# Moving layer norm 1's scale and shift ahead of the transposes, with adds on GpSimd, in an encoder block on one core

## The chip, the core and the metric

The kernel runs on one core of a Trainium2 chip. The metric is device microseconds of one execution, the median of several runs; lower is better. TensorE does the matrix products and the transposes, VectorE (DVE), ScalarE (ACT) and GpSimd (POOL) the work on single elements, SyncE (SP) issues the transfers.

## What is computed

One encoder block on 256 tokens of width 2048 and 16 meta tokens, in float32. The part around the change is the end of the mixer and the start of the feed-forward part:

```python
def layer_norm(x, g, b):
    mu = jnp.mean(xf, axis=-1, keepdims=True)
    var = jnp.mean(jnp.square(xf - mu), axis=-1, keepdims=True)
    y = (xf - mu) * lax.rsqrt(var + LN_EPS)
    return y * g + b
...
        mix = jnp.concatenate([o_hg, o_ret], axis=-1) @ w_out[layer]
        h = layer_norm(DEEPNORM_ALPHA * h + mix, ln1_g[layer], ln1_b[layer])
        ff = (jax.nn.silu(h @ w_gate[layer]) * (h @ w_up[layer])) @ w_down[layer]
        h = layer_norm(DEEPNORM_ALPHA * h + ff, ln2_g[layer], ln2_b[layer])
```

So `h` is needed twice: as the operand of the gate and up products (feature-major, after a transpose) and as the residual of the second sum (token-major, as it comes).

## The kernel before

**Precision.** Each weight block of 128 x 2048 floats is fetched into one of three `raw` buffers and split into a rounded high part `whi` (a cast on ACT, L77) and the rest `wlo` (a subtraction on DVE, L78), three buffers each. Activations are split the same way. A product is then three matmuls: high by high, high by low, low by high.

**Token groups.** `token_group` makes 512 output columns for both tiles of 128 tokens (tile 0 and tile 1). Its argument `order` lists pairs (tile i, weight block g); for each pair TensorE issues 12 matmuls (4 pieces of 128 rows, three matmuls each, L133). After a tile's last pair `evac` reads the sum out of PSUM. After every second piece, that is every six matmuls, `tick()` is called: it takes the next entry of the list `steps` once it has been passed over as many times as the entry's number says.

**Layer norm 1.** After the last quarter of the output projection, `add_up` adds tile i's result into `acc` (token-major) on DVE (L740, L742 for the statistics) and calls `ln1_tile(i)`. That forms mean and variance (L212, L184), the power -0.5 on GpSimd (L186), the shift (L214), and normalizes the four chunks c0 to c3 of 512 columns, in place (L770 on ACT, L218 on DVE). Each chunk then becomes a step: four transposes on TensorE into one PSUM bank (L237), four ACT instructions that scale and shift each 128 columns with a per-partition gain and bias (L227), a cast to the high part of `h` on ACT (L231), a subtraction for the low part on DVE (L232). The residual `acc` gets the same gain and bias a second time, token-major, on DVE, by the entries of `later` (L777, L778) with rows of gain and bias that were copied to all partitions (`gb`).

**Gate and up.** `first_hidden` runs a token group for the first 512 columns of gate, in the order (0,0), (0,1), (0,2), (1,0), (1,1), (1,2), (0,3), (1,3), then one for up. The chunks of tile 1 are transposed while TensorE works on tile 0 of the gate group.

**Order.** A scheduling pass fixes the order on each engine when the program is built; on the chip each engine works through its own list strictly in that order and waits where an operand is not ready.

Of the kernel before, what the change touches and what calls it, by code (L numbers as in the profile page):

```python
# [9 lines left out]
F32 = mybir.dt.float32  # L10
# [3 lines left out]
ALU = mybir.AluOpType  # L14
AX = mybir.AxisListType

P = 128
# [14 lines left out]
ALPHA = 2.0 ** 0.25  # L32
# [3 lines left out]
C_LB, C_HG, C_RG, C_RB, C_IG, C_IB, C_1G, C_1B = 0, 16, 24, 32, 40, 56, 72, 88  # L36
# [4 lines left out]
def encoder_kernel(ctx: ExitStack, tc: tile.TileContext, x, meta, par, rows, w_in, w_out,  # L41
                   w_gu, w_down, masks, rope, dtab, out):
    nc = tc.nc
# [9 lines left out]
    def bank(c):  # L53
        return pss.tile([P, 512], F32, name="sc") if c % 2 else psm.tile([P, 512], F32, name="ms")


    def fetch(src, parts=1):
        raw = rawp.tile([P, 2048], F32, name="raw")
        w = 2048 // parts
        for p in range(parts):  # L60
            nc.sync.dma_start(raw[:, p * w:(p + 1) * w], src[:, p * w:(p + 1) * w])
        return raw, parts
# [1 line left out]
    def new_split():  # L64
        return (splitp.tile([P, 2048], F32R, name="whi"), splitp.tile([P, 2048], F32R, name="wlo"))

    def split(fetched, dst=None):
        hi, lo = dst or new_split()
        split_parts(fetched, hi, lo, 0, 2048)
        return hi, lo  # L70

    def split_parts(fetched, hi, lo, c0, c1):
        raw, parts = fetched
        w = 2048 // parts
        for c in range(c0, c1, w):
            sl = slice(c, c + w)
            nc.scalar.copy(hi[:, sl], raw[:, sl])  # L77
            nc.vector.tensor_tensor(out=lo[:, sl], in0=raw[:, sl], in1=hi[:, sl].bitcast(F32), op=ALU.subtract)  # L78

    def load_block(src):  # L80
        return split(fetch(src))


    soon, steps = [], deque()
# [18 lines left out]
    def token_group(blocks, operand, order, evac, split_of=None, halve=False):  # L103

        ps = [psp.tile([P, 512], F32, name="pp") for _ in range(2)]
        ws, left, seen = {}, [sum(1 for t, _ in order if t == i) for i in range(2)], [0, 0]
        for i, g in order:  # L110
            if g not in ws:
                ws[g] = split_of(g) if split_of else load_block(blocks[g])
            whi, wlo = ws[g]
            left[i] -= 1
            if halve and i:
                if left[i]:
                    continue
                n = len(ws)
                for half in range(2):
                    ph = psp.tile([P, 512], F32, name="pp")  # L120
                    for k in range(4 * n):
                        a_hi, a_lo = operand(i, k)
                        c = (k % 4) * 512 + half * 256
                        for m, (a, w) in enumerate(((a_hi, 0), (a_hi, 1), (a_lo, 0))):
                            nc.tensor.matmul(ph[:, :256], a, ws[k // 4][w][:, c:c + 256],  # L125
                                             start=(k == 0 and m == 0), stop=(k == 4 * n - 1 and m == 2))
                    evac(i, ph[:, :256], half)
                continue
            for j in range(4):
                k = 4 * g + j  # L130
                a_hi, a_lo = operand(i, k)
                for m, (a, w) in enumerate(((a_hi, whi), (a_hi, wlo), (a_lo, whi))):
                    nc.tensor.matmul(ps[i], a, w[:, j * 512:(j + 1) * 512],  # L133
                                     start=(seen[i] == 0), stop=(left[i] == 0 and j == 3 and m == 2))
                    seen[i] = 1
                if j % 2:
                    tick()
            if left[i] == 0:
                if halve:
                    evac(i, ps[i][:, :256], 0)  # L140
                    evac(i, ps[i][:, 256:], 1)
                else:
                    evac(i, ps[i])
# [33 lines left out]
    ident = cpool.tile([P, P], F32, name="ident")  # L177
# [32 lines left out]
    def moments(mom, rstd, shift, st, np_):  # L210

        nc.vector.bn_aggr(out=mom[:np_], in_=st[:np_])  # L212
        rsqrt(rstd[:np_], mom[:np_, 1:2], 1, np_, LN_EPS)
        nc.vector.tensor_scalar(out=shift[:np_], in0=mom[:np_, 0:1], scalar1=rstd[:np_], scalar2=-1.0,  # L214
                                op0=ALU.mult, op1=ALU.mult)
# [18 lines left out]
    def transposed_chunk(src, c, pool, cg, cb, hs, ls, on_act):  # L234
        pt = bank(c)
        for k in range(4):
            nc.tensor.transpose(pt[:, k * P:(k + 1) * P], src[:, (4 * c + k) * P:(4 * c + k + 1) * P], ident)  # L237
        affine_split(pt, pool, cg, cb, c, hs, ls, on_act)
# [126 lines left out]
    with tc.tile_pool(name="att", bufs=1) as att:  # L365
# [349 lines left out]
        acc, gb = big[:, :2], big[:, 2:]  # L715
# [21 lines left out]
        def add_up(n, scale, stats, done=None):  # L737
            def evac(i, ps):
                sl = acc[:, i, n * 512:(n + 1) * 512]
                nc.vector.scalar_tensor_tensor(out=sl, in0=sl, scalar=scale, in1=ps, op0=ALU.mult, op1=ALU.add)  # L740
                if stats:
                    nc.vector.bn_stats(out=lst[:, i, n, :], in_=sl)  # L742
                if done:
                    done(i)
            return evac
# [11 lines left out]
    ffp = ctx.enter_context(tc.tile_pool(name="ffp", bufs=1))  # L757
    hp = ctx.enter_context(tc.tile_pool(name="hp", bufs=1))
    h = hp.tile([P, KC, 2, SEQ], F32R, name="h")

    later = []

    def ln1_tile(i):
        moments(lm[:, i], lr[:, i], ls[:, i], lst[:, i, :4], P)
        for c in range(4):
            sl = acc[:, i, c * 512:(c + 1) * 512]
            if i == 0 and c < 2:
                normalize(sl, sl, lm[:, i, 0:1], lr[:, i])
            else:
                nc.scalar.activation(sl, sl, AF.Identity, scale=lr[:, i], bias=ls[:, i])  # L770

        def chunk(c):
            transposed_chunk(acc[:, i], c, ffp, C_1G, C_1B, h[:, 4 * c:4 * c + 4, 0, i * P:(i + 1) * P], h[:, 4 * c:4 * c + 4, 1, i * P:(i + 1) * P], 4)

        def affine(c):
            sl = slice(c * 512, (c + 1) * 512)
            nc.vector.tensor_tensor(out=acc[:, i, sl], in0=acc[:, i, sl], in1=gb[:, 0, sl], op=ALU.mult)  # L777
            nc.vector.tensor_tensor(out=acc[:, i, sl], in0=acc[:, i, sl], in1=gb[:, 1, sl], op=ALU.add)  # L778
        steps.append((3, lambda: chunk(0)))
        for c in range(1, 4):  # L780
            steps.append((1, lambda c=c: chunk(c)))
        later.extend((2, lambda c=c: affine(c)) for c in range(4))

    row_bcast(2, gb[:, 0])
    row_bcast(3, gb[:, 1])
    with tc.tile_pool(name="spare", bufs=1) as spare:
        def held(g):
            dst = None
            if g == 3:
                dst = (spare.tile([P, 2048], F32R, name="shi"), spare.tile([P, 2048], F32R, name="slo"))  # L790
            return split(fetch(w_out[12 + g]), dst)

        def done(i):
            ln1_tile(i)
        token_group(None, halves(mhi, mlo), [(0, 0), (1, 0), (0, 1), (0, 2), (0, 3), (1, 1), (1, 2), (1, 3)],
                    add_up(3, ALPHA, True, done), held)
    hid = [actp.tile([P, 2, 8, SEQ], F32R, name=f"t{i}", tag="mix", bufs=2) for i in range(2)]
    fpool = ctx.enter_context(tc.tile_pool(name="fpool", bufs=1))
    hid.append(fpool.tile([P, 2, 8, SEQ], F32R, name="t2"))
# [27 lines left out]
    def first_hidden():  # L827

        gate = [None, None]

        def gate_evac(i, ps):
            gate[i] = g = ffp.tile([P, 512], F32, name="gate", tag="w", bufs=6)
            nc.scalar.activation(g, ps, AF.Sigmoid)
            nc.vector.tensor_tensor(out=g, in0=ps, in1=g, op=ALU.mult)

        def up_evac(i, ps):
            t = gate[i]
            nc.vector.tensor_tensor(out=t, in0=ps, in1=t, op=ALU.mult)

            def turn():  # L840
                pt = bank(i)
                for k in range(4):
                    nc.tensor.transpose(pt[:, k * P:(k + 1) * P], t[:, k * P:(k + 1) * P], ident)
                pv = pt.rearrange("p (k t) -> p k t", k=4)
                hi = hid[0][:, 0, :4, i * P:(i + 1) * P]
                nc.scalar.copy(hi, pv)
                nc.vector.tensor_tensor(out=hid[0][:, 1, :4, i * P:(i + 1) * P], in0=pv, in1=hi.bitcast(F32),
                                        op=ALU.subtract)
            soon.append([2, turn])
        token_group([w_gu[g] for g in range(4)], h_op,  # L850
                    [(0, 0), (0, 1), (0, 2), (1, 0), (1, 1), (1, 2), (0, 3), (1, 3)], gate_evac)
        steps.extend(later)
        token_group([w_gu[4 + g] for g in range(4)], h_op, alternate(4), up_evac)

    def hidden(f, s):
# [158 lines left out]
```

## Time and profile before

| | |
|---|---|
| median of 3 runs | 1289.88 us (1289.38 to 1291.33) |
| the profiled execution, own time | 1288.35 us |
| its span on the core | 1286.6 us |
| TensorE busy | 98% of the span |
| DVE, ACT, GpSimd busy | 59%, 43%, 1% |

The profiled execution lies 1.5 us below the median. TensorE is busy for nearly all of the span, so what counts in any other engine's work is only where TensorE has to wait for it. Chunk names c0 to c3 and tile numbers below are those of the section above; "gate group" is the token group of the first gate columns.

### The profile page before, as it was taken

What the parts mean: (1) busy time and instruction counts of PE and PEld (TensorE: products, weight loads), DVE (VectorE), ACT (ScalarE), POOL (GpSimd) and SP (SyncE); (2) the same over time, 40 slices, a digit from 0 to 9 for tenths busy, and PEclk for the clock granted to TensorE, in tenths of its full rate; (3) what the DMA queues carried; (4) which work ended last, traced back from release to release, by engine and by line L of the source; (5) the groups of instructions that cost most, each with busy time, mean ns of one, the idle gap of its engine ahead of it and who ended that gap; (6) DMA issues with size and microseconds to landing.
All of it is one profiled execution on the core that took longest, in us unless ns stands there. A gap on an engine that the chain in (4) does not pass through costs nothing.

```text
span 1286.6 us, 17123 instructions
## 1 busy us (share of the span) xinstructions
PE 1261.6 (98%) x7260; PEld 1111.8 (86%) x7260; DVE 757.9 (59%) x888; ACT 554.0 (43%) x586; POOL 13.6 (1%) x26
## 2 busy tenths in 40 slices
PE   6999999999999999999999999999999999999996
PEld 4989999898999888878888888888888888888886
DVE  7765575565566685775555555444455555554565
ACT  7634434443444343564444444433344444444340
POOL 0000000000000000000000000000000000000000
PEclk9999999999999999999999999999999999999998
DMA  6644444444434477465555555555555555555541
GB/s 234 252 154 161 164 159 139 162 164 164 164 136 160 154 304 256 169 235 198 189 197 195 180 185 194 184 189 190 192 208 184 194 197 186 181 189 191 190 175 66
DMA packets 34956, 237.53 MB, mean 185 GB/s; under 512 B 4016, under 2 KB 4656, under 8 KB 6960
## 3 DMA queue, kind: packets, MB, share of 16 engines
q1 hardware_dynamic: 34880, 236.44, 51.9%
q8 instruction: 57, 0.93, 0.3%
q14 instruction: 19, 0.16, 0.0%
HBM read 234.33 MB, written 2.10 MB: 184 GB/s over the span
## 4 chain that ended last, share of the span: by engine, by line
PE 95%; DVE 2%; ACT 1%; issue 1%; DMA 0%; POOL 0%; SPq 0%; POOLq 0%; DVEq 0%
PE pp L133 33%; PE pp L863 23%; PE pp L321 15%; PE pp L868 12%; PE pp L332 5%; PE pp L337 2%; PE sc L463 1%; PE pp L125 1%; PE sc L645 1%; DMA raw<-in_w_in_dram 0%; DVE wlo L78 0%; ACT fl L227 0%; PE ms L575 0%; PE ms L572 0%; PE ms L657 0%
## 5 line engine op out<-in xcount | busy, mean ns | idle before, releaser
L78 DVE TENSOR_TENSOR wlo<-raw,whi 128x2048 fp32r<-128x2048 f32 (+1 forms) x211 | 478.8, 2270 | 390.1 <-ACT whi L77 382.7
L77 ACT CAST whi<-raw 128x2048 fp32r<-128x2048 f32 (+1 forms) x211 | 399.5, 1893 | 407.4 <-PE pp L133 201.1
L863 PE MATMUL pp<-h,whi 128*128 128x512 f32 x1280 | 305.4, 391 | 0.0
L863 PEld LDWEIGHTS pp<-h,whi 128*128 128x128 f32 x1280 | 235.3, 188 | 45.6
L133 PE MATMUL pp<-whi,t 128*128 128x512 f32 x648 | 200.0, 389 | 0.0
L321 PE MATMUL pp<-xx,whi 128*128 128x272 f32 x1024 | 199.7, 290 | 0.0
L868 PEld LDWEIGHTS pp<-h,wlo 128*128 128x128 f32 x1280 | 164.0, 191 | 6.2
L868 PE MATMUL pp<-h,wlo 128*128 128x256 f32 x1280 | 166.1, 283 | 0.0
L321 PEld LDWEIGHTS pp<-xx,whi 128*128 128x128 f32 x1024 | 162.3, 188 | 0.5
L321 PE MATMUL pp<-xx,wlo 128*128 128x272 f32 x512 | 146.8, 287 | 0.0
L133 PEld LDWEIGHTS pp<-whi,t 128*128 128x128 f32 x648 | 121.6, 188 | 25.3
L133 PE MATMUL pp<-wlo,t 128*128 128x512 f32 x324 | 126.1, 389 | 0.0
L321 PEld LDWEIGHTS pp<-xx,wlo 128*128 128x128 f32 x512 | 96.5, 188 | 0.2
L133 PE MATMUL pp<-whi,xx 128*128 128x512 f32 x256 | 85.6, 405 | 2.0 <-ACT xx L231 1.9
L133 PEld LDWEIGHTS pp<-wlo,t 128*128 128x128 f32 x324 | 60.8, 188 | 12.5
L332 PE MATMUL pp<-xx,whi 128*128 128x512 f32 x256 | 63.5, 396 | 0.0
L133 PEld LDWEIGHTS pp<-whi,xx 128*128 128x128 f32 x256 | 48.9, 192 | 13.5 <-ACT xx L231 2.8
L332 PEld LDWEIGHTS pp<-xx,whi 128*128 128x128 f32 x256 | 47.0, 188 | 9.0
L133 PE MATMUL pp<-wlo,xx 128*128 128x512 f32 x128 | 51.0, 398 | 0.1
L133 PE MATMUL pp<-whi,mhi 128*128 128x512 f32 x120 | 46.9, 391 | 0.0
L133 PE MATMUL pp<-whi,mlo 128*128 128x512 f32 x120 | 46.7, 389 | 0.0
L133 PE MATMUL pp<-wlo,mhi 128*128 128x512 f32 x120 | 46.7, 389 | 0.0
(207 smaller groups left out, 996.9 us busy)
## 6 DMA issues: line engine op xcount, KB each, us to landing
raw<-in_w_gu_dram SPq DMA_DIRECT2D x88, 1024.0 KB, 4.9
raw<-in_w_in_dram SPq DMA_DIRECT2D x62, 1024.0 KB, 4.9
raw<-in_w_down_dram SPq DMA_DIRECT2D x44, 1024.0 KB, 4.9
raw<-in_w_out_dram SPq DMA_DIRECT2D x16, 1024.0 KB, 4.9
acc<-in_rows_dram SPq DMA_DIRECT2D x6, 1024.0 KB, 7.4
raw<-in_w_in_dram SPq DMA_DIRECT2D x4, 512.0 KB, 8.3
acc<-in_x_dram SPq DMA_DIRECT2D x2, 1024.0 KB, 6.0
out_dram<-acc SPq DMA_DIRECT2D x6, 256.0 KB, 2.3
```

Source lines behind the costliest of these rows:

```text
L77: nc.scalar.copy(hi[:, sl], raw[:, sl])
L78: nc.vector.tensor_tensor(out=lo[:, sl], in0=raw[:, sl], in1=hi[:, sl].bitcast(F32), op=ALU.subtract)
L125: nc.tensor.matmul(ph[:, :256], a, ws[k // 4][w][:, c:c + 256], start=(k == 0 and m == 0), stop=(k == 4 * n - 1 and m == 2))
L133: nc.tensor.matmul(ps[i], a, w[:, j * 512:(j + 1) * 512], start=(seen[i] == 0), stop=(left[i] == 0 and j == 3 and m == 2))
L321: nc.tensor.matmul(ps[:, :T], w[:, kc, :], a[:, kc, XM:], start=(kc == 0 and j == 0), stop=(kc == KC - 1 and j == 2))
L332: nc.tensor.matmul(ps.rearrange("p (m t) -> p m t", m=2), hi[:, kc, :], xx[:, kc, :, X0:], start=(kc == 0), stop=False)
L337: nc.tensor.matmul(ps[:, :SEQ], lo[:, kc, :], xhi[:, kc, X0:], start=False, stop=(kc == KC - 1))
L463: nc.tensor.matmul(sc[:, c * 192:(c + 1) * 192], K[:, (o + c) * P:(o + c + 1) * P], E[:, :, (o + c) * 64:(o + c + 1) * 64], start=True, st ...
L645: nc.tensor.matmul(sc[:, c0:c0 + n], RK[:, k, k0:k0 + P], RQ[:, k, q0:q0 + n], start=(k == 0), stop=(k == 1))
L863: nc.tensor.matmul(ps, hi[:, kc, :], h[:, kc].rearrange("p m t -> p (m t)"), start=(kc == 0), stop=False)
L868: nc.tensor.matmul(ps[:, :SEQ], lo[:, kc, :], h[:, kc, 0, :], start=False, stop=(kc == KC - 1))
```

## The change

Layer norm 1's gain and bias are applied once, token-major, before the transposes: DVE multiplies each chunk of `acc` by the gain row (L773), and the bias row is added by DVE for c0 and by GpSimd for c1 to c3 (L774). The transposed chunk is then split straight from PSUM: one cast on ACT (L785), one subtraction on DVE (L786). `later` is gone. Only c0 of tile 0 is normalized on DVE, all others on ACT. A chunk's first step waits for four ticks in place of three. The gate group takes all four weight blocks for tile 0, then all four for tile 1; for that, block 3's split goes into a buffer of its own (the later `t2`), behind c0's add on DVE, and block 2 is fetched and split in two halves, with the low part of one half made on GpSimd and the other on DVE. The evacuation of the last quarter of the projection has a higher priority in the scheduling pass.

```diff
-    def split_parts(fetched, hi, lo, c0, c1):
+    def split_parts(fetched, hi, lo, c0, c1, *engines):
...
-            nc.vector.tensor_tensor(out=lo[:, sl], in0=raw[:, sl], in1=hi[:, sl].bitcast(F32), op=ALU.subtract)
+            (engines[c // w] if engines else nc.vector).tensor_tensor(out=lo[:, sl], in0=raw[:, sl], in1=hi[:, sl].bitcast(F32), op=ALU.subtract)
...
-            if i == 0 and c < 2:
+            if i == 0 and c == 0:
                 normalize(sl, sl, lm[:, i, 0:1], lr[:, i])
             else:
                 nc.scalar.activation(sl, sl, AF.Identity, scale=lr[:, i], bias=ls[:, i])
+            nc.vector.tensor_tensor(out=sl, in0=sl, in1=gb[:, 0, cols], op=ALU.mult)
+            m = (nc.gpsimd if c else nc.vector).tensor_tensor(out=sl, in0=sl, in1=gb[:, 1, cols], op=ALU.add)
+            if c == 0:
+                begun[:] = [m.ins]
 
         def chunk(c):
-            transposed_chunk(acc[:, i], c, ffp, C_1G, C_1B, h[:, 4 * c:4 * c + 4, 0, i * P:(i + 1) * P], h[:, 4 * c:4 * c + 4, 1, i * P:(i + 1) * P], 4)
-
-        def affine(c):
-            sl = slice(c * 512, (c + 1) * 512)
-            nc.vector.tensor_tensor(out=acc[:, i, sl], in0=acc[:, i, sl], in1=gb[:, 0, sl], op=ALU.mult)
-            nc.vector.tensor_tensor(out=acc[:, i, sl], in0=acc[:, i, sl], in1=gb[:, 1, sl], op=ALU.add)
-        steps.append((3, lambda: chunk(0)))
+            pt = bank(c)
+            for k in range(4):
+                kc = 4 * c + k
+                nc.tensor.transpose(pt[:, k * P:(k + 1) * P], acc[:, i, kc * P:(kc + 1) * P], ident)
+            pv = pt.rearrange("p (k t) -> p k t", k=4)
+            part = h[:, 4 * c:4 * c + 4, :, i * P:(i + 1) * P]
+            nc.scalar.copy(part[:, :, 0, :], pv)
+            nc.vector.tensor_tensor(out=part[:, :, 1, :], in0=pv, in1=part[:, :, 0, :].bitcast(F32), op=ALU.subtract)
+        steps.append((4, lambda: chunk(0)))
         for c in range(1, 4):
             steps.append((1, lambda c=c: chunk(c)))
-        later.extend((2, lambda c=c: affine(c)) for c in range(4))
...
+        def evac(i, ps):
+            with tc.high_priority():
+                sum_up(i, ps)
...
+        def gate_split(g):
+            flat = hid[2].rearrange("p m k t -> p (m k t)")
+            if g == 2:
+                return split(fetch(w_gu[g], 2), None, nc.gpsimd, nc.vector)
+            if g == 3:
+                with tc.issue_after(begun[0]):
+                    return split(fetch(w_gu[g]), (flat[:, :2048], flat[:, 2048:]))
+            return split(fetch(w_gu[g]))
...
-        token_group([w_gu[g] for g in range(4)], h_op,
-                    [(0, 0), (0, 1), (0, 2), (1, 0), (1, 1), (1, 2), (0, 3), (1, 3)], gate_evac)
-        steps.extend(later)
+        token_group(None, h_op, [(i, g) for i in range(2) for g in range(4)], gate_evac, gate_split)
```

On every engine the order before this stage and after the up group is the same in both programs, and TensorE issues the same number of matmuls and transposes.

On DVE, from tile 0's normalization to tile 1's multiplications, the list before reads as follows (`acc<-acc` at L777 and L778 are the gain and bias of the residual; `h<-fl` is a low part of `h`):

```order
L218 TENSOR_SCALAR acc<-acc,lm,lr 128x512 x2
L777 TENSOR_TENSOR acc<-acc 128x512
L778 TENSOR_TENSOR acc<-acc 128x512
L78 TENSOR_TENSOR wlo<-raw,whi 128x2048
L232 TENSOR_TENSOR h<-fl,h 128x4x128
L777 TENSOR_TENSOR acc<-acc 128x512 x2
L232 TENSOR_TENSOR h<-fl,h 128x4x128
L740 SCALAR_TENSOR_TENSOR acc<-acc,pp 128x512
L778 TENSOR_TENSOR acc<-acc 128x512
L232 TENSOR_TENSOR h<-fl,h 128x4x128
L742 BN_STATS lst<-acc 128x6
L778 TENSOR_TENSOR acc<-acc 128x512
```

In the changed program the same stretch of DVE's list reads:

```order
L773 TENSOR_TENSOR acc<-acc 128x512 x2
L774 TENSOR_TENSOR acc<-acc 128x512
L773 TENSOR_TENSOR acc<-acc 128x512 x2
L78 TENSOR_TENSOR wlo<-raw,whi 128x2048
L786 TENSOR_TENSOR h<-ms,h 128x4x128
L786 TENSOR_TENSOR h<-sc,h 128x4x128
L740 SCALAR_TENSOR_TENSOR acc<-acc,pp 128x512
L78 TENSOR_TENSOR wlo<-raw,whi 128x1024
L742 BN_STATS lst<-acc 128x6
L786 TENSOR_TENSOR h<-ms,h 128x4x128
L212 BN_AGGR lm<-lst 128x2
L786 TENSOR_TENSOR h<-sc,h 128x4x128
```

The multiplications of tile 0 now stand at the head, block 1's low part behind them, and the half of block 2's low part between tile 1's sum (L740) and its statistics (L742).

GpSimd's list had only the two powers here; in the changed program it reads:

```order
L186 TENSOR_TENSOR lr<-rst,nhalf 128x1
L774 TENSOR_TENSOR acc<-acc 128x512 x3
L78 TENSOR_TENSOR wlo<-raw,whi 128x1024
L186 TENSOR_TENSOR lr<-rst,nhalf 128x1
L774 TENSOR_TENSOR acc<-acc 128x512 x3
```

Tile 0's three adds and the half block stand ahead of tile 1's power, and tile 1's three adds behind it.

On TensorE, the transposes of tile 1 (into the banks `ms` and `sc`) stood like this in the gate group before:

```order
L237 MATMUL ms<-ident,acc 128x128 x4
L237 MATMUL sc<-ident,acc 128x128 x4
L237 MATMUL ms<-ident,acc 128x128 x4
L133 MATMUL pp<-wlo,h 128x512
L133 MATMUL pp<-whi,h 128x512 x2
L133 MATMUL pp<-wlo,h 128x512
L133 MATMUL pp<-whi,h 128x512 x2
L133 MATMUL pp<-wlo,h 128x512
L133 MATMUL pp<-whi,h 128x512 x2
L133 MATMUL pp<-wlo,h 128x512
L133 MATMUL pp<-whi,h 128x512
L237 MATMUL sc<-ident,acc 128x128 x4
```

In the changed program they stand like this (`t` is block 3's buffer):

```order
L782 MATMUL ms<-ident,acc 128x128 x4
L133 MATMUL pp<-whi,h 128x512
L133 MATMUL pp<-wlo,h 128x512
L133 MATMUL pp<-whi,h 128x512 x2
L133 MATMUL pp<-wlo,h 128x512
L133 MATMUL pp<-whi,h 128x512
L782 MATMUL sc<-ident,acc 128x128 x4
L133 MATMUL pp<-t_4872,h 128x512
L782 MATMUL ms<-ident,acc 128x128 x4
L782 MATMUL sc<-ident,acc 128x128 x4
L133 MATMUL pp<-t_4872,h 128x512 x11
```

Tile 1's c0 stands after 25 matmuls of the gate group before and after 30 now (and after tile 0's c3, which moved behind the group's first six matmuls); c1 follows six matmuls later, c2 one more, c3 right behind c2.

## Rows read from the trace of the kernel before

**Rows 1.** The page: span, and engines' busy time.
```profile
span 1286.6 us, 17123 instructions
...
PE 1261.6 (98%) x7260; PEld 1111.8 (86%) x7260; DVE 757.9 (59%) x888; ACT 554.0 (43%) x586; POOL 13.6 (1%) x26
```
**Rows 2.** Waits, TensorE, whole span: waiter, releaser, us in total, times, longest.
```profile
PE sc L237 <- DVE xt L218: 9.5, 1, 9.5
...
PE ms L237 <- ACT acc L770: 1.5, 1, 1.5
```
**Rows 3.** Timeline, TensorE: start us, us, line, tiles, shape, count, idle before.
```profile
530.89 0.39 PE L133 MATMUL pp<-whi,mhi 128*128 128x512 f32 x1
...
534.75 0.39 PE L133 MATMUL pp<-whi,mlo 128*128 128x512 f32 x1
534.98 0.60 PE L237 MATMUL ms<-ident,acc 128*128 128x128 f32 x4
...
536.11 0.40 PE L133 MATMUL pp<-whi,mhi 128*128 128x512 f32 x1
...
546.15 0.62 PE L133 MATMUL pp<-whi,h 128*128 128x512 f32 x2
548.25 0.66 PE L237 MATMUL ms<-ident,acc 128*128 128x128 f32 x4 [1.47 <-ACT acc L770]
...
568.21 0.62 PE L133 MATMUL pp<-whi,h 128*128 128x512 f32 x2
...
588.38 0.39 PE L133 MATMUL pp<-wlo,h 128*128 128x512 f32 x1
...
588.84 0.60 PE L843 MATMUL ms<-ident,gate 128*128 128x128 f32 x4
```
**Rows 4.** Windows, the stretch of the wait: busy us of PE, PEld, DVE, ACT, POOL; clock.
```profile
547.00:550.00 3.00, 1.65 (x11) 1.18 (x12) 2.87 (x3) 2.62 (x4) 0.10 (x1) 1.00 0.02 5
```
**Rows 5.** Timeline, DVE, around both tiles' statistics and at the kernel's end.
```profile
531.09 0.69 DVE L740 SCALAR_TENSOR_TENSOR acc<-acc,pp 128x512 f32<-128x512 f32 x1 [3.92 <-PE pp L133]
531.81 0.69 DVE L742 BATCH_NORM_STATS2 lst<-acc 128x6 f32<-128x512 f32 x1
...
533.66 0.21 DVE L214 TENSOR_SCALAR ls<-lm,lr 128x1 f32<-128x1 f32 x1 [0.67 <-POOL lr L186]
...
545.99 0.69 DVE L778 TENSOR_TENSOR acc<-acc 128x512 f32<-128x512 f32 x1
547.13 0.21 DVE L214 TENSOR_SCALAR ls<-lm,lr 128x1 f32<-128x1 f32 x1 [0.45 <-POOL lr L186]
...
547.86 2.28 DVE L78 TENSOR_TENSOR wlo<-raw,whi 128x2048 fp32r<-128x2048 f32 x1
550.06 1.28 DVE L777 TENSOR_TENSOR acc<-acc 128x512 f32<-128x512 f32 x2
...
1263.33 0.74 DVE L821 SCALAR_TENSOR_TENSOR acc<-acc,lm 128x512 f32<-128x512 f32 x1
```
**Rows 6.** Timeline, GpSimd: a memory fill, and three of the powers.
```profile
39.13 0.53 POOL L380 MEMSET SM<- 128x512 f32 x1
...
533.08 0.56 POOL L186 TENSOR_TENSOR lr<-rst,nhalf 128x1 f32<-128x1 f32 x1 [83.93 <-DVE rst L184]
546.09 1.00 POOL L186 TENSOR_TENSOR lr<-rst,nhalf 128x1 f32<-128x1 f32 x1 [12.46 <-DVE rst L184]
1263.58 0.90 POOL L186 TENSOR_TENSOR lr<-rst,nhalf 128x1 f32<-128x1 f32 x1 [716.49 <-DVE rst L184]
```
**Rows 7.** Timeline, ACT: a weight cast, four normalizations, a cast from PSUM.
```profile
535.34 1.89 ACT L77 CAST whi<-raw 128x2048 fp32r<-128x2048 f32 x1
...
547.38 2.93 ACT L770 ACTIVATE acc<-acc,ls,lr 128x512 f32<-128x512 f32 x4 [0.70 <-DVE ls L214]
...
590.85 0.58 ACT L846 CAST t<-ms 128x512 fp32r<-128x512 f32 x1
```
**Rows 8.** One line's instructions, the weight casts and subtractions: duration ns least, median, most.
```profile
L77 ACT CAST whi<-raw x211: 1032/1907/1983, 9.5 to 1247.7; 128x2048 fp32r<-128x2048 f32 x104, 128x1024 fp32r<-128x1024 f32 x2
L78 DVE TENSOR_TENSOR wlo<-raw,whi x211: 1186/2292/2294, 10.6 to 1250.9; 128x2048 fp32r<-128x2048 f32 x104, 128x1024 fp32r<-128x1024 f32 x2
```

More of the change, by code (lines that the diff above doesn't have):

```diff
@@ L65, in new_split, with split @@
         return (splitp.tile([P, 2048], F32R, name="whi"), splitp.tile([P, 2048], F32R, name="wlo"))
-    def split(fetched, dst=None):
+    def split(fetched, dst=None, *engines):
         hi, lo = dst or new_split()
-        split_parts(fetched, hi, lo, 0, 2048)
+        split_parts(fetched, hi, lo, 0, 2048, *engines)
         return hi, lo
-    def split_parts(fetched, hi, lo, c0, c1):
+    def split_parts(fetched, hi, lo, c0, c1, *engines):
         raw, parts = fetched
@@ L759, in encoder_kernel @@
     h = hp.tile([P, KC, 2, SEQ], F32R, name="h")
-    later = []
+    begun = []
     def ln1_tile(i):
@@ L765, in ln1_tile @@
         for c in range(4):
-            sl = acc[:, i, c * 512:(c + 1) * 512]
-            if i == 0 and c < 2:
+            cols = slice(c * 512, (c + 1) * 512)
+            sl = acc[:, i, cols]
+            if i == 0 and c == 0:
                 normalize(sl, sl, lm[:, i, 0:1], lr[:, i])
@@ L791, in held @@
             return split(fetch(w_out[12 + g]), dst)
-        def done(i):
-            ln1_tile(i)
+        sum_up = add_up(3, ALPHA, True, ln1_tile)
+        def evac(i, ps):
+            with tc.high_priority():
+                sum_up(i, ps)
         token_group(None, halves(mhi, mlo), [(0, 0), (1, 0), (0, 1), (0, 2), (0, 3), (1, 1), (1, 2), (1, 3)],
-                    add_up(3, ALPHA, True, done), held)
+                    evac, held)
     hid = [actp.tile([P, 2, 8, SEQ], F32R, name=f"t{i}", tag="mix", bufs=2) for i in range(2)]
```

## Prediction, made before the changed kernel ran

> **What bounds the kernel now.** The page comes first: TensorE is busy for 1261.6 of 1286.6 us, no other engine for more than 60% [rows 1]. So the change is worth what it does to TensorE's waits, and the list of these comes next: 9.5 us once at the start, which the change does not reach, and 1.5 us at tile 1's transposes of layer norm 1, the place of the change [rows 2].
>
> The timeline says what that place loses in all. From the projection's first matmul for tile 1 (530.89) to the end of up (the next transposes, 588.84) are 57.95 us, with 36 + 96 + 96 = 228 matmuls and 8 groups of four transposes [rows 3]. Undisturbed, 89 matmuls start between 568.21 and 588.38, one per 0.2266 us; from 534.75 to 536.11 stand four matmuls and one group, so a group costs 1.36 - 0.91 = 0.45 us [rows 3]. 228 x 0.2266 + 8 x 0.45 = 55.3 us. The stage loses 57.95 - 55.3 = **2.7 us**, most of it between the matmuls at 546.15 and the transposes at 548.25, where ACT's normalization is late. The granted clock stays at 1.00, the 2.4 GHz level, around that wait [rows 4], so the wait costs its own length. No change to this stage can gain more than 2.7 us unless TensorE gets less work, and its counts stay.
>
> **What is removed and added.** Per chunk, ACT loses four scalings and keeps one cast, 0.58 us from PSUM [rows 7]; DVE loses nothing in number, since multiplication, addition and subtraction were there before, but multiplication and addition now stand in front of the transposes. None of this is on TensorE; it costs by the time at which each chunk is ready. Three things make chunks later (gain, bias, and the wait for both) and two make them due later: one tick more (six matmuls, 1.36 us) and a gate group in which tile 1 is not needed for 48 matmuls in place of 36.
>
> The prices: a DVE operation of 512 columns 0.69 us, 0.6 in a row; a whole low part 2.28 [rows 5], half of it 1.19; half a cast 1.03 [rows 8], a whole one 1.89; a normalization on ACT 0.73 in a row (2.93 for four) [rows 7]; the power 0.56 when undisturbed [rows 6]. GpSimd's add of 512 columns stands in no row. From below, a fill of as many columns takes 0.53 us [rows 6]; from above I take three such passes, two reads and a write, 1.6 us. I use two passes, 1.1 us, since the write can go along with the reads, and 2.1 us for the half block. The Trainium skill's GPSIMD Engine Reference, section Elementwise, gives 4497 ns for an add of 2048 columns; by an estimate from that, 1.12 us and 2.25 us, every sum below would grow by less than half a microsecond. No run here shows that figure yet.
>
> **The walk, if no engine holds up another.** I keep TensorE's list and lay the others beside it.
> - Tile 0: the shift is there at 533.87 [rows 5]. DVE normalizes c0 to 534.3, multiplies c0 and c1 to 535.7, adds c0 to 536.3. TensorE comes to c0's transposes 24 matmuls after 530.89, at 536.3: no wait. GpSimd adds c1, c2, c3 to 536.8, 538.0, 539.1; they are due at 538.1, 540.0 and, in the gate group, 541.8. That group starts at 530.89 + 36 x 0.2266 + 3 x 0.45 = 540.4.
> - Tile 1: the sum L740 stands behind block 1's low part (its cast ends at 538.0, so it ends at 540.3) and two low parts of h, and starts at 541.5. Then half a low part, the statistics, two more low parts of h: 545.5. Power, shift, normalization, multiplication, addition: c0 is ready at 545.5 + 0.6 + 0.25 + 0.85 + 0.7 + 0.7 = 548.6. It is due at 540.4 + 30 x 0.2266 + 0.45 = 547.65: TensorE waits **1.0 us**.
> - c1 is added in time; c2 and c3 come from GpSimd 1.1 us apart, but are due 0.68 and 0.45 us after the chunk before: 0.4 + 0.65 us.
>
> Sum 2.1 us of waits against 2.7: a gain of **0.6 us**. Everything else is covered: the low parts of tile 1's h are needed only after tile 0's last 11 matmuls; the casts of up's weights wait for tile 1's first pair to free a buffer, which leaves three pairs, 8.2 us, for 1.89 + 2.28 us; the rows of gain and bias for layer norm 2 are fetched in SP's list behind tile 1's adds, ahead of up's last weights, whose product is some 20 us off. If that cover were gone, each late block would show as a wait at up.
>
> **Does GpSimd work beside DVE?** The powers say no. The same 128 x 1 operation takes 0.56 us at 533.08, when DVE waits, but 1.00 us at 546.09 and 0.90 us at 1263.58 [rows 6]. Each time a DVE operation with both inputs in SBUF had just begun, at 545.99 and 1263.33, and ended at 546.68 and 1264.07 [rows 5]; each time the power ends 0.41 us behind that. So GpSimd stood still until DVE was through. Both new kinds of GpSimd work meet such DVE work all along: multiplications, c0's add, and block 1's, 2's and 3's low parts.
>
> With GpSimd held behind DVE and DVE never held (**one-sided**), the walk becomes: c0's add and c2's and c3's multiplications keep DVE to 537.5, so c1's add ends at 538.6 (due 538.1: 0.45); the low part of block 1 runs from 538.0 to 540.3, so c2's ends at 541.4 (due 540.4: 1.0). In tile 1, the multiplications and right behind them block 3's low part keep DVE from 548.6 to 552.7; c1 is added at 553.8, due at 550.9 (2.9); c2 and c3 follow (0.4 + 0.65). Sum 5.4, less 2.7: **2.8 us slower**.
>
> The Trainium skill's page SBUF — State Buffer, section Who interferes with whom, says that it goes both ways: a DVE operation with two SBUF inputs and a GpSimd one that reads SBUF exclude each other for a whole instruction, and the first to issue goes first. The rows here agree for GpSimd behind DVE (+0.41 us twice); no row shows DVE behind GpSimd.
>
> As a mechanism of this kernel, **both ways** would be: DVE's multiplications of tile 0 alternate with GpSimd's adds to 539.75, block 1's low part ends at 542.05 and c0's low part of h at 542.6, due at 540.85: 1.8. The half blocks exclude each other, tile 1's c0 is ready at 551.7, due 549.45: 2.2. c1 and c2 wait 0.6 and 1.1; block 3's low part comes between c2's and c3's adds, 2.95. Sum 8.65, 6.0 slower. If each hands over before its row ends (rows of DVE overlap by 0.1 us) and GpSimd's first 0.15 us need no access (0.56 - 0.41), the same walk gives 6.1 of waits, **3.5 slower**.
>
> So being held costs 2.8 to 6.0 us. I take 3.5, where the one-sided walk and the gentler two-sided one come close. With adds of 0.53 and 1.6 us in place of 1.1 the held walks give 1.2 and 10 us at their ends.
>
> **How it is set against the runs.** 3.5 us on the profiled execution's own 1288.35 is 1291.9; the median of the runs shown is 1.5 us above that execution, so I forecast 1289.9 + 3.5 = **1293.4**. A measurement of this kernel tells some 0.2%, 2.6 us, from no change.
>
> **The rivals.**
> - *Side by side.* GpSimd's operations of hundreds of columns pass between DVE's, and only tiny ones show a hold. Then 0.6 us is gained, 1289.3 (1288.9 to 1290.8 over the bounds of the add). For it: only two powers speak for the hold. Against it: both end at the same 0.41 us.
> - *Held, but cheaply.* Adds near the fill's 0.53 us: 1.2 to 1.8 us slower, 1291.4. Against it: two operands are read.
> - *All waits vanish.* Tile 1's chain needs no four scalings per chunk on ACT and less in front of it on DVE. If the sum L740 starts at 540.6 rather than 541.5, and adds take at most 0.7 us, c0 is ready when due and the whole 2.7 us are gained: 1287.2. Against it: block 1's low part stands in front of L740, and only its cast, whose buffer the projection frees, could come earlier. It decides at a start of L740 before 540.6.
> - *Held and slow.* Adds of 1.6 us: 5 to 10 us slower, 1297.
>
> **How the numbers follow.** Held with adds of 0.8 to 1.3 us, the forecast, 0.45; its own range is 1291.8 to 1296.5. Side by side 0.27; held, but cheaply 0.11; all waits vanish 0.09; held and slow 0.08. Slower by over 0.2% are the last and most of the first: 0.08 + 0.39 = 0.47. Faster by over 0.2% needs all of the 2.7 us: 0.09. Within: 0.44. The range from 1288.3 to 1296.5 leaves out the vanished waits and the slow adds, and some tail.
>
> **What would show it.** Right: GpSimd's adds last beyond 1.1 us where a multiplication or low part runs on DVE, or DVE's beyond 0.69; TensorE waits at tile 1's c1 or c3 for a GpSimd add, with block 3's low part just before it; the stage from tile 1's first matmul to the transposes behind up takes some 61.5 us in place of 57.95. Wrong: adds that keep one length whatever DVE does, waits of 2 us or less in sum, or a wait at up's first weights, which I hold for covered.

## The result and the profile after

The changed kernel takes **1296.52 us** (median of 6 runs, 1295.97 to 1298.08) against 1289.63 for the kernel before (6 runs beside them): a ratio of 1.0057, with a 95% interval of 1.0047 to 1.0067. It is slower, as forecast, but 3.1 us over the forecast and just outside its range. The profiled execution took 1296.79 us.

TensorE has the same 7260 matmuls as before. It counts as busy for 3 us more, as it runs slower for a while, and the span is 8 us longer [rows 1]:

```profile
span 1294.8 us, 17103 instructions
...
PE 1264.8 (98%) x7260; PEld 1113.9 (86%) x7260; DVE 758.4 (59%) x881; ACT 544.1 (42%) x556; POOL 28.8 (2%) x33
```

The list of TensorE's waits between 525 and 600 us (columns as in [rows 2]) has three entries where the kernel before had one:

```profile
PE sc L782 <- POOL acc L774: 2.4, 1, 2.4
PE ms L782 <- issue: 2.1, 1, 2.1
PE pp L133 <- DVE h L786: 1.4, 1, 1.4
```

On TensorE's timeline they stand at tile 0's c0 (its low part of `h`), tile 1's c0 and tile 1's c3. The one put down to "issue" ends with DVE's add of tile 1's c0 (L774, 551.57 to 552.26):

```profile
531.54 0.39 PE L133 MATMUL pp<-whi,mhi 128*128 128x512 f32 x1
...
543.18 0.73 PE L133 MATMUL pp<-whi,h 128*128 128x512 f32 x2 [1.44 <-DVE h L786]
...
552.36 0.63 PE L782 MATMUL ms<-ident,acc 128*128 128x128 f32 x4 [2.06 <-issue]
...
559.61 0.66 PE L782 MATMUL sc<-ident,acc 128*128 128x128 f32 x4 [2.36 <-POOL acc L774]
560.02 4.36 PE L133 MATMUL pp<-t,h 128*128 128x512 f32 x11
...
596.90 0.60 PE L862 MATMUL ms<-ident,gate 128*128 128x128 f32 x4
```

The stage of the prediction, from the projection's first matmul for tile 1 to the transposes behind up, runs from 531.54 to 596.90: 65.36 us, 7.4 more than before [rows 3]. Its start is another 0.65 us later than before, which no part of the change touches; over the profiles of all runs here it lies between 530.4 and 531.9 us.

The eleven matmuls at 560.02 take 4.36 us; at the 0.2266 us of the undisturbed stretch, with the last one's tail, they would take some 2.7. The windows (stretch; its length and TensorE's busy time; instructions; granted clock; DMA share; GB/s) say why:

```profile
553.00:554.00 1.00, 1.00 (x5) 0.75 0.00 0
554.00:555.00 1.00, 1.00 (x4) 0.50 0.00 0
555.00:556.00 1.00, 1.00 (x6) 0.50 0.00 0
556.00:557.00 1.00, 0.96 (x5) 0.55 0.48 197
...
560.00:561.00 1.00, 1.00 (x6) 0.66 0.81 262
561.00:562.00 1.00, 1.00 (x3) 0.50 1.03 426
562.00:563.00 1.00, 1.00 (x4) 0.50 1.09 426
563.00:564.00 1.00, 1.00 (x5) 0.63 0.94 393
```

Twice the granted clock falls to 0.50, the 1.2 GHz level, once behind the wait of 2.06 us and once behind that of 2.36. Before, it stayed at 1.00 around its one wait [rows 4].

DVE and GpSimd show what makes the chunks late. DVE (compare [rows 5]):

```profile
536.83 2.39 DVE L773 TENSOR_TENSOR acc<-acc 128x512 f32<-128x512 f32 x2
539.15 3.38 DVE L78 TENSOR_TENSOR wlo<-raw,whi 128x2048 fp32r<-128x2048 f32 x1
542.45 0.68 DVE L786 TENSOR_TENSOR h<-ms,h 128x512 fp32r<-128x512 f32 x1
...
544.24 2.87 DVE L78 TENSOR_TENSOR wlo<-raw,whi 128x1024 fp32r<-128x1024 f32 x1
...
552.18 2.97 DVE L773 TENSOR_TENSOR acc<-acc 128x512 f32<-128x512 f32 x3
555.07 3.36 DVE L78 TENSOR_TENSOR t<-raw,t 128x2048 fp32r<-128x2048 f32 x1
```

GpSimd (compare [rows 6]):

```profile
536.45 1.62 POOL L774 TENSOR_TENSOR acc<-acc 128x512 f32<-128x512 f32 x1 [2.16 <-DVE acc L773]
538.70 4.96 POOL L774 TENSOR_TENSOR acc<-acc 128x512 f32<-128x512 f32 x2 [0.64 <-DVE acc L773]
543.63 2.40 POOL L78 TENSOR_TENSOR wlo<-raw,whi 128x1024 fp32r<-128x1024 f32 x1
549.15 0.56 POOL L186 TENSOR_TENSOR lr<-rst,nhalf 128x1 f32<-128x1 f32 x1 [3.13 <-DVE rst L184]
552.94 6.61 POOL L774 TENSOR_TENSOR acc<-acc 128x512 f32<-128x512 f32 x3 [3.23 <-DVE acc L773]
```

Read the two side by side from 538.70. GpSimd starts c2's add while DVE still multiplies to 539.2. Block 1's low part starts on DVE at 539.15 and shows 3.38 us where it took 2.28 [rows 5]: 1.1 us, about one add, longer. It ends at 542.53. GpSimd's row, c2's and c3's adds, ends at 543.66, 1.13 us behind that. So DVE stood still for c2's add, and c3's add stood still for DVE. The two multiplications ahead of that are longer by c1's add, 2.39 us for the pair where the kernel before shows 1.28 [rows 5]. The same holds at 555.07: 3.36 us on DVE, and three adds that last 6.61 us on GpSimd. The subtraction for `h` at 542.45 falls into c3's add, yet takes its usual 0.68 us; one of its two inputs is in PSUM.

### The profile page after: what moved, and what is told of

Read it like the earlier page. It is cut to its first block, busy times and chain, and to the rows that moved or that the text cites. A ratio compares the mean times of both kernels' runs of the same rounds, so it can differ in the third digit from the quotient of the medians.

```text
span 1294.8 us, 17103 instructions
## 1 busy us (share of the span) xinstructions
PE 1264.8 (98%) x7260; PEld 1113.9 (86%) x7260; DVE 758.4 (59%) x881; ACT 544.1 (42%) x556; POOL 28.8 (2%) x33
## 4 chain that ended last, share of the span: by engine, by line
PE 88%; issue 8%; DVE 2%; POOL 1%; DMA 1%; SPq 0%; ACT 0%; POOLq 0%; DVEq 0%
PE pp L133 26%; PE pp L880 23%; PE pp L321 15%; PE pp L885 12%; PE pp L332 4%; PE pp L337 2%; PE sc L463 1%; PE pp L125 1%; POOL acc L774 1%; DVE wlo L78 1%; PE sc L645 1%; DMA raw<-in_w_in_dram 1%; DVE acc L773 0%; PE ms L575 0%; PE ms L572 0%
```

## The experiments

Theory X: a DVE operation with two inputs in SBUF and a GpSimd one exclude each other for a whole operation, both ways, and this makes all of the loss. Rival G: the gate group's new order and the later steps lose. Rival L: the adds on GpSimd are only longer than DVE's and late; DVE is not held. Theory C, formed on the trace after: standing still costs TensorE its clock on top of the wait. Ratios are against the kernel before on the same chip, with 95% intervals.

**All adds and low parts on DVE.** The changed kernel without GpSimd's new work:

```diff
-            m = (nc.gpsimd if c else nc.vector).tensor_tensor(out=sl, in0=sl, in1=gb[:, 1, cols], op=ALU.add)
+            m = nc.vector.tensor_tensor(out=sl, in0=sl, in1=gb[:, 1, cols], op=ALU.add)
...
-                return split(fetch(w_gu[g], 2), None, nc.gpsimd, nc.vector)
+                return split(fetch(w_gu[g], 2))
```

> The changed kernel with every bias add and the whole of block 2's low part on DVE; GpSimd keeps only the powers. Theory X (GpSimd's and DVE's operations with two inputs in SBUF exclude each other both ways): all held operations go, waits in the stage fall to some 1.6 us in sum (1.0 at tile 1's c0, 0.2 and 0.35 at c2 and c3), so about 1 us faster than before: ratio 0.999, 0.998 to 1.001, TensorE's clock at 1.00 through the stage, low parts of 2048 columns at 2.29 us. Rival G (the new gate order, and chunks due later in the list, cost the time): it stays as slow as the changed kernel, ratio 1.005. Rival L (GpSimd's adds are only long, 1.15 us, and nothing excludes anything): DVE's six further adds take 3.6 us, the chunks come about as late as from GpSimd, ratio 1.002 to 1.004.

Measured: 1288.39 us, ratio 0.9995 (0.9986 to 1.0004), stage 57.57 us. TensorE's whole list of waits between 528 and 592 us:

```profile
PE ms L782 <- issue: 0.4, 1, 0.4
PE ms L782 <- DVE acc L774: 0.4, 1, 0.4
```

Block 1's low part on DVE, and the window behind tile 1's c0 (columns as in [rows 4]):

```profile
539.33 2.28 DVE L78 TENSOR_TENSOR wlo<-raw,whi 128x2048 fp32r<-128x2048 f32 x1
550.00:556.00 6.00, 5.56 (x30) 4.08 (x29) 6.00 (x9) 2.52 (x5) 0.00 (x0) 1.00 0.95 363
```

The whole loss is gone with GpSimd's work, while order, steps and transposes are still the changed kernel's; the low part is back at 2.28 us and the clock at 1.00. As a cause of the 7 us, G falls. L, which gave 1.002 to 1.004, falls too.

**Only the half low part back on DVE.** The second pair of lines above, alone.

> The changed kernel with only the half block given back to DVE; the adds stay on GpSimd. Theory X: the half on GpSimd held DVE's own half for 1.7 us, that goes, but DVE has 1.2 us more to do; the adds still exclude the multiplications and block 3's low part, so about 3 to 4.5 us slower than before, ratio 1.0025 to 1.0035, with waits at tile 0's c0 (1.5 us) and at tile 1's c3 (2 to 2.5 us). Rival L: the half matters little, ratio 1.004 to 1.006. Rival G: unchanged, 1.005 to 1.006.

Measured: 1296.38 us, 1.0057 (1.0045 to 1.0070), stage 65.19: no gain where X expected 3 to 4 us, and the ratio that L and G gave. Tile 1's c0 does wait for 0.9 us only. Tile 1's c3:

```profile
558.64 1.12 PE L782 MATMUL sc<-ident,acc 128*128 128x128 f32 x4 [2.61 <-POOL acc L774]
```

The windows around it (columns as above) show a longer stretch at the lower clock:

```profile
556.00:562.00 6.00, 3.39 (x11) 0.54 0.85 314
562.00:568.00 6.00, 6.00 (x25) 0.89 0.37 154
```

c3 comes 27.3 us after the stage's start (531.32) where the changed kernel has 28.1, so 0.75 us are saved up to there, not 3. Behind it the stage takes 37.9 us in place of 37.3: most of what was saved goes back at the lower clock. X's sum over separate waits does not hold; that DVE and GpSimd hold one another, its rows show as before (block 1's low part again 3.38 us).

**Adds on GpSimd in the kernel before.** There the residual's add (L778) hangs on nothing that TensorE waits for:

```diff
-            nc.vector.tensor_tensor(out=acc[:, i, sl], in0=acc[:, i, sl], in1=gb[:, 1, sl], op=ALU.add)
+            nc.gpsimd.tensor_tensor(out=acc[:, i, sl], in0=acc[:, i, sl], in1=gb[:, 1, sl], op=ALU.add)
```

> The kernel before with one edit: the eight bias adds of the residual (L778), for which nothing in this stage waits, go from DVE to GpSimd. Theory X: nobody waits for them, yet each shuts DVE's multiplications and low parts out for some 1.1 us, so that rows of DVE of 0.69 and 2.29 us grow by about 1.1 where an add runs, tile 1's shift comes about 2 us later, and the kernel is 1.5 to 4 us slower, ratio 1.001 to 1.003. Rival L: DVE has eight operations (4.8 us) less and keeps its lengths, tile 1's chain comes earlier, 0.5 to 1.5 us faster, ratio 0.999. The two have opposite signs.

Measured: 1291.49 us, 1.0014 (1.0005 to 1.0023). DVE has eight operations less and is later all the same: tile 1's variance (L184) is 15.8 us into the stage in place of 15.0. Two of DVE's rows:

```profile
541.20 1.79 DVE L777 TENSOR_TENSOR acc<-acc 128x512 f32<-128x512 f32 x1
...
543.51 1.40 DVE L232 TENSOR_TENSOR h<-fl,h 128x512 fp32r<-128x512 f32 x1
```

Both take 0.68 to 0.69 us undisturbed. An add for which nothing in this stage waits still holds DVE. L, by which this would have been a gain, falls. Tile 1's power, which now stands behind such an add on GpSimd, adds 0.2 us to the delay. The size is small: 0.14%.

**No adds for c1 to c3 at all.** The changed kernel with block 2's low part on DVE and the bias adds of columns 512 to 2047 left out, so that part of the output lacks the bias.

> The changed kernel without the bias adds of layer norm's columns 512 to 2047 in both tiles (they are left out, so the output lacks that shift), and with block 2's low part wholly on VectorE; all else, the gate's order and the fourth block's place too, is the changed kernel's. Theory X (all of the loss comes from GpSimd's five kinds of work beside VectorE's): VectorE's rows go back to 0.69, 1.2 and 2.29 us, the granted clock stays at 1.00, the stage takes 55.8 to 57 us, a ratio of 0.998 to 0.9993; against the run with all adds on VectorE the adds' own 1.8 us on tile 1's chain are gained in part. Rival G (the other edits lose on their own): waits of 1 us or more stay ahead of tile 1's blocks, and the ratio is 1.000 or more.

Measured: 1287.39 us, 0.9990 (0.9981 to 0.9999), stage 56.78, one wait of 0.9 us at tile 1's c0. That is X's range. Even with adds that cost nothing, this arrangement would gain only some 0.1%: 1 us below all adds on DVE by the medians, 0.6 by the ratios.

**The gate's order alone.** The kernel before, with the gate group tile by tile and block 3 in its own buffer:

```diff
-        token_group([w_gu[g] for g in range(4)], h_op,
-                    [(0, 0), (0, 1), (0, 2), (1, 0), (1, 1), (1, 2), (0, 3), (1, 3)], gate_evac)
+            return split(fetch(w_gu[g]), (flat[:, :2048], flat[:, 2048:]) if g == 3 else None)
...
+        token_group(None, h_op, [(i, g) for i in range(2) for g in range(4)], gate_evac, gate_split)
```

> The kernel before with the new gate order alone: all four blocks for tile 0, then tile 1, block 3 split into its own buffer; layer norm 1 as it was. Theory X: tile 1's c0 is still due after 25 matmuls and ready as late as before (1.6 us), but c1 to c3 stand further apart, so 0 to 1 us faster, ratio 0.9990 to 1.000. Rival G: slower by 3 us or more, ratio above 1.002.

Measured: 1291.07 us, 1.0013 (1.0004 to 1.0022), neither theory's number. ACT's timeline says what this edit did besides:

```profile
547.25 1.97 ACT L77 CAST t<-raw 128x2048 fp32r<-128x2048 f32 x1
549.05 2.99 ACT L770 ACTIVATE acc<-acc,ls,lr 128x512 f32<-128x512 f32 x4
```

Block 3's cast, which has its buffer early now, stands in front of tile 1's normalizations (549.05 in place of 547.38 [rows 7]). Tile 1's c0 waits for 2.5 us, and the clock of 550 to 556 us falls to 0.72. In the changed kernel the same cast runs from 541.35 to 543.26, well ahead of tile 1's normalizations, which start at 550.00, so it is not in their way there.

**Tile 1's c2 and c3 later.** The changed kernel, with TensorE's transposes of tile 1 held at their place in the program, which in the trace puts c2 and c3 8 and 14 matmuls behind c1 (six and twelve of tile 0's, and two of tile 1's that come in between):

```diff
+        def placed(c):
+            if not i:
+                return chunk(c)
+            with tc.issue_after(newest[0]):
+                chunk(c)
+
-        steps.append((4, lambda: chunk(0)))
+        steps.append((4 if i else 4, lambda: placed(0)))
         for c in range(1, 4):
-            steps.append((1, lambda c=c: chunk(c)))
+            steps.append((1, lambda c=c: placed(c)))
```

(`newest` holds the last matmul issued.)

> The changed kernel, with one move: tile 1's third and fourth blocks of transposes stand 6 and 12 matmuls of the gate behind the second, where in the changed kernel they stood 1 matmul behind it, one directly after the other; no operation is added or left out. Theory X (both kinds of instruction hold one another, so the columns come late, and TensorE waits where a block of transposes stands too early): the waits of the third and the fourth block (about 0.84 and 2.36 us) are filled by 12 matmuls of 2.7 us, which is about 3 us less; those of the first and second block (2.06 and 0.65 us) stay, and with them some of the drop of the granted clock. That gives 1292.5 to 1294 us, a ratio of 1.002 to 1.0035. Rival L (the late columns only hand the delay on to the low parts of h and to the gate's product, on which the end hangs anyway): the stage stays at 64.5 us or more, a ratio of 1.0045 or more.

Measured: 1294.25 us, 1.0035 (1.0022 to 1.0049), stage 62.70. That is at X's edge, and L falls, but the way is not X's: c3's wait is gone and another took its place. TensorE's waits between 528 and 600 us:

```profile
PE pp L133 <- DVE t L78: 2.5, 1, 2.5
PE ms L782 <- issue: 2.0, 1, 2.0
PE pp L133 <- DVE h L786: 1.4, 1, 1.4
PE sc L782 <- POOL acc L774: 0.3, 1, 0.3
```

With c2 and c3 out of the way, the matmuls of block 3 are next, and they wait for block 3's low part, which stands on DVE between the held adds. The waits of the list sum to 6.3 us, those of the changed kernel to 5.9. The stage is 65.36 - 62.70 = 2.7 us shorter all the same, as the granted clock of this execution stayed at 1.00 throughout: some 1.7 us of that are the eleven matmuls behind c3, which took 4.36 us at the lower clock in the changed kernel, and about 1 us is left for the move. All five executions have a mean granted clock of 0.996 or 0.997, all six of the changed kernel 0.994. With waits of 2.0 and 2.5 us and no fall, the length of a wait alone does not decide whether the clock falls.

**TensorE busy while it waits.** The same with 18 transposes of the identity ahead of tile 1's c0, and then with 24 more ahead of block 3's first matmul:

```diff
+            if i == 1 and c == 0:
+                for k in range(18):
+                    nc.tensor.transpose(pt[:, :P], ident, ident)
...
+                with tc.issue_after(newest[0]):
+                    pt = bank(1)
+                    for k in range(24):
+                        nc.tensor.transpose(pt[:, :P], ident, ident)
```

> The same as the run before with its moved transposes, and with 18 small transposes of the identity matrix into the PSUM bank ahead of tile 1's first block (they are overwritten by that block), so that TensorE works through most of the 2.06 us in which it stood waiting there. They take about 2 us and wait for nothing. Theory C (the granted clock falls to 0.8 behind that wait because TensorE stood still): the granted clock stays at 1.00 from 550 to 562 us, the matmuls behind the wait take 0.227 us each, and the time is 0.7 to 1.5 us under that of the run before. Rival D (the clock falls for another reason, as the work of VectorE and GpSimd beside it): the granted clock falls as before, and the time is the same or up to 0.3 us over that of the run before.

Measured with the first 18: 1297.64 us, 1.0053 (1.0040 to 1.0065); single executions at 1297.66, 1297.64, 1297.74 (mean granted clock 0.994 to 0.995) and at 1294.40 and 1295.23 (0.997 and 0.996). In the profiled one, which is one of the three, the clock stays at 1.00 through the filled wait, and falls behind the next, block 3's, of 2.9 us:

```profile
550.00:556.00 6.00, 5.55 (x36) 1.00 0.28 117
556.00:562.00 6.00, 3.14 (x10) 0.65 0.75 287
562.00:568.00 6.00, 6.00 (x24) 0.78 0.57 238
```

C had promised 0.7 to 1.5 us under the run before, D at most 0.3 over it; it is 3.4 over, so neither has the number. Against the changed kernel the fall has moved one wait on; in the run before, whose five executions lie under 1295 us, there was none. Hence the second run:

> The run with 18 small transposes ahead of tile 1's first block, and 24 more (about 2.7 us, into a PSUM bank that nobody reads) ahead of the first matmul with the gate's fourth weight block, where TensorE stood for 2.5 to 2.9 us until that block's low part was there. In the run before, three of five executions took 1297.7 us at a mean granted clock of 0.994 to 0.995, the others 1294.4 and 1295.2 us at 0.997 and 0.996. Theory C (the clock falls to half because TensorE stands still): with both waits filled the granted clock stays at 1.00 from 550 to 568 us in the profile, no execution is at 1297 us or more, and all lie between 1293.3 and 1295 us. Rival D (the clock falls whatever TensorE does there): windows at 0.5 appear again in about every second execution, and the median is 1295 us or more.

Measured: 1294.45 us, 1.0046 (1.0033 to 1.0060), five executions from 1293.51 to 1295.33, none near 1297. The same stretch in its profile:

```profile
556.00:562.00 6.00, 5.68 (x37) 1.00 0.86 314
562.00:568.00 6.00, 6.00 (x28) 1.00 0.46 193
```

C's main signs are there: the clock stays at 1.00 in the profile from 550 to 568 us, and no execution comes near the 1297.7 us of the three above, which cost 2.4 to 3.3 us over the two beside them. Its upper end of 1295 us was passed twice (1295.23 and 1295.33), and one execution, of 1294.38 us, has a mean granted clock of 0.995, the level of those three. So C is borne out, but not shown: five executions stand against five, and the run with no useless work at all had no fall in five either. GpSimd's share in D is out: in the run with the gate's order alone and in two of the three tries below GpSimd has nothing but powers, and the clock falls there too, to 0.72, 0.50 and 0.61 over six us behind or around waits of 2.5, 3.4 and 5.4. In time the useless work wins nothing over the run that had only waited at a full clock (1294.25).

**Three tries for a faster kernel.** First, all adds on DVE with tile 1's transposes about 12 matmuls later (the `placed` of above, with 6 ticks for tile 1's c0):

> The changed kernel with all adds and block 2's half low part on VectorE (as in the run with all on VectorE), and with tile 1's four blocks of transposes 12, 12, 6 and 6 matmuls later. Theory X: with no held instruction left, the two waits of 0.43 and 0.42 us that stayed there are filled, nothing new appears, and the stage goes from 57.6 to between 55.5 and 56.9 us: a ratio of 0.998 to 0.999. Rival L (the chain over VectorE sets the end: the low parts of tile 1's h come so much later that the gate's matmuls wait for them instead): a wait of 0.4 us or more ahead of tile 1's gate matmuls, and a ratio of 0.9995 or more.

Measured: 1295.45 us, 1.0047 (1.0034 to 1.0059). Without the transposes, TensorE is at block 3's first matmuls before their low part is there, and waits for 5.4 us (L's ratio and its kind of wait, of another operand than expected). DVE works through adds and multiplications from 548.61 without a gap and only then comes to that low part:

```profile
553.43 2.28 DVE L78 TENSOR_TENSOR t<-raw,t 128x2048 fp32r<-128x2048 f32 x1
```

Second, the kernel before with the tile by tile gate, block 3's split issued behind tile 1's normalizations, and later transposes of tile 1:

> The kernel before with two things: the gate group tile by tile, its fourth block in a buffer of its own and cast behind tile 1's normalizations; and tile 1's four blocks of transposes about 12 matmuls later. Layer norm's scale and shift stay behind the transposes, on ScalarE. Theory X: the waits of 1.47 us and less that the kernel before shows ahead of tile 1's transposes go, and the 2.7 us that the stage loses today come back in part: 1287 to 1288.5 us, a ratio of 0.998 to 0.9995. Rival G (the order of the gate group itself costs, through the fourth block's cast and low part, as in the run with the gate's order alone): the fourth block's low part or tile 1's high parts come late, waits of 1 us or more appear in the gate group, and the ratio is 1.000 to 1.002.

Measured: 1291.84 us, 1.0016 (1.0007 to 1.0025). That is G's ratio. The wait at c0 is gone; this one stands at block 2's matmuls instead:

```profile
PE pp L133 <- DVE wlo L78: 3.4, 1, 3.4
```

The low part starts at 547.94, before at 547.86 [rows 5], where the wait for c0 had covered it. Third, all on DVE with the gate's old order, so that block 3 has time, and tile 1's c0 to c3 after 30, 37, 43 and 49 matmuls:

> The changed kernel's layer norm rows ahead of the transposes and its split from PSUM, with all adds and low parts on VectorE, with the gate group in the order of the kernel before (the fourth block of weights comes last), and with tile 1's four blocks of transposes 30, 37, 43 and 49 matmuls behind tile 0's last one. Theory X: VectorE's row of work between 540 and 556 us loses the fourth block's low part of 2.29 us, which now has time until the gate's seventh part; TensorE waits at most about 0.5 us ahead of tile 1's first block, and the stage takes 55.8 to 56.8 us: 1287.4 to 1288.4 us, a ratio of 0.9983 to 0.9992. Rival L (with tile 1's columns later, the low parts of h end the wait of the second half): a wait of 0.5 us or more ahead of tile 1's gate matmuls, and a ratio of 0.9995 or more.

Measured: 1291.20 us, 1.0015 (1.0006 to 1.0024). c0 waits for 0.4 us, as expected, but TensorE then waits for tile 1's first low part of `h`, as L had it. DVE has that low part only behind tile 1's eight multiplications and adds, which run from 548.04 to 552.9:

```profile
553.60 0.73 PE L133 MATMUL pp<-whi,h 128*128 128x512 f32 x2 [1.53 <-DVE h L786]
...
552.86 0.68 DVE L786 TENSOR_TENSOR h<-ms,h 128x512 fp32r<-128x512 f32 x1
```

None of the three beats the kernel before. The best complete version is the one with all adds on DVE, which can't be told from it.

## Why the prediction was off

- *What bounds the kernel, and where the change acts* held: the loss is in the one stage, 65.36 - 57.95 = 7.4 us, in TensorE's waits and, behind them, in its clock.
- *Does GpSimd work beside DVE?* It does not, and it goes **both ways**, and no row before had shown that: 2.28 became 3.38 and 3.36 on DVE. That is what the Trainium skill's page SBUF — State Buffer, section Who interferes with whom, says; the trace agrees. *Side by side*, *held, but cheaply* and *all waits vanish* are out.
- *The price of an add*, 1.1 us, was right: 1.13 from DVE's end at 542.53 to GpSimd's at 543.66. *Held and slow*, which gave 1297 for adds of 1.6 us, named nearly the right time for a wrong reason. The half block took 2.40, not 2.1. Two differences are 0.1 too high: 5.4 - 2.7 is 2.7, not 2.8, and 6.1 - 2.7 is 3.4, not 3.5.
- **The step that failed** is the last of the working: "So being held costs 2.8 to 6.0 us. I take 3.5". The gentler walk, in which each engine hands over before its row ends and GpSimd's first 0.15 us need no access, is not what these rows show. The full one is, nearly: tile 0's low part was to wait 1.8 us and waited 1.44, tile 1's c0 2.2 and 2.06, c3 2.95 and 2.36, in the very places and order. At c1 and c2 it had 0.6 and 1.1, and the list shows none, as TensorE itself came there late at the lower clock. The held operations add up to whole ones in the rows (1.1 + 2.28 = 3.38). Two powers with the same 0.41 us behind DVE were the only evidence, and they could not tell how a long operation behaves.
- **A term that was missing**: "the granted clock stays at 1.00 around that wait, so the wait costs its own length" was carried from one wait of 1.47 us to waits of over 2. The windows from 560 to 564 us lack 0.34 + 0.50 + 0.50 + 0.37 = 1.7 us of full clock, those from 553 to 557 another 1.7. The latter lie ahead of tile 1's c3, whose add ends at 559.55 and hangs on DVE's and GpSimd's rows alone, so they cost nothing of their own. With one such stretch the full walk's stage is 55.3 + 8.65 + 1.7 = 65.65 us, and 65.36 were measured; its time is 1289.9 + 6.0 + 1.7 = 1297.6, against 1296.5. The one execution profiled before also hid that the clock varies: of 63 executions of the kernel before that ran beside the experiments, ten have a mean granted clock of 0.994 or 0.995 and take 1290.5 to 1293.0 us, while the others' median is 1288.9. No trace shows where in the kernel that happens.
- *Everything else is covered* held in the changed kernel: no wait at up. The later runs show how thin it is at block 3, whose low part is the next thing late as soon as c2 and c3 are not.

Left open: why the clock fell behind 2.06 us in the changed kernel and did not fall behind 2.04 and 2.49 in the profile with c2 and c3 later, and whether it was the useless work that kept it up.

## What to carry to other kernels

In these runs GpSimd was no spare VectorE for operations on two SBUF inputs: wherever VectorE had such operations of its own at that time, what was moved came back as time on VectorE, operation by operation, and at the places where VectorE was late already. Where the evidence on contention has a gentle and a harsh reading, walk the harsh one to the end and give it the weight until a long operation has been seen beside another. A wait that is removed by moving work on TensorE is worth only what the next operand on the same engine allows, so look up when that one is ready before moving anything.

## What the runs showed of the hardware

- The exclusion takes turns by whole operations: with both engines' lists full, one operation of each follows the other, and the row of the one that waits grows by the other: 2.28 to 3.38 us on DVE behind one add of 1.13, and three adds in 6.61 us on GpSimd. DVE's operations with an input in PSUM ran beside a GpSimd add or half block at their usual 0.67 to 0.68 us.
- A stand-still of 2 to 3 us in a busy stretch can be followed by a few microseconds of TensorE at the 1.2 GHz level, but need not be: it was in the changed kernel's profile behind 2.06 and 2.36 us, and not behind 2.04 and 2.49 with c2 and c3 later. By their times, three of five executions of one program had it, and two had not.
- GpSimd's power for 128 values took 0.56 us in the changed kernel, when DVE was idle, and 1.47 with all adds on DVE, where a half low part of 1.22 us ran on DVE at that time.
